# Split weights at eight different distances modulo 256 bytes from the operands they are multiplied with

## The chip, the cores and the metric

The kernel runs on one core of a Trainium2 chip. The metric is the device time in microseconds of one execution. Smaller is better. The core has a matrix engine (TensorE, PE in the profile, with its weight loads as PEld), three engines for elementwise work (VectorE or DVE, ScalarE or ACT, GpSimd or POOL) and a queue that issues transfers (SyncE or SP). Operands lie in an on-chip memory of 128 partitions; a tile occupies the same bytes of every partition, so its place is one start address in bytes.

## The reference

One block of a streaming encoder, on x of 256 tokens by 2048 features, all in float32:

```python
x = x + 0.5 * swiglu(rms_norm(x, ffn1_norm), ffn1_w_up, ffn1_w_down)     # 2048 -> 2 x 5632 -> 2048
h = rms_norm(x, mix_norm)
q_a, f_a, i_a, g_a, x_b, gate_b, gates = split(h @ w_in)
y_a = rms_norm(hgrn2(q_a, f_a, i_a)) * silu(g_a)                         # gated linear recurrence
y_b = rglru(conv4(x_b)) * gelu(gate_b)                                   # scan over the tokens
g = sigmoid(gates + b_gate)
x = x + (g[0] * (y_a @ w_branch_a) + g[1] * (y_b @ w_branch_b)) @ w_out
x = x + cross_attention(rms_norm(x), rms_norm(mem), wq, wkv, wo)         # 4 heads, 256 memory tokens
x = x + 0.5 * swiglu(rms_norm(x, ffn2_norm), ffn2_w_up, ffn2_w_down)
return rms_norm(x, final_norm)
```

Nearly all of the work is products of x or something made of it (256 rows) with large weight matrices, each of which is read once from DRAM.

## The kernel before, in words

**Split products.** TensorE multiplies a type called float32r here, which is faster than float32 and keeps fewer bits. To keep float32's accuracy each operand is split in two: a high part, which is the operand rounded to float32r (`h`, written by ScalarE, L155), and a low part, the operand less its high part (`l`, written by VectorE, L156). A product of A and B is then high x high + low x high + high x low, summed in the accumulators. The operands made of x are split once and kept: `xh` and `xl` in the feed-forward stages, `ops` in the middle, where the two parts lie side by side in one tile, `hidop` for the hidden layer.

**Weight tiles.** A weight tile is 128 partitions by 2048 elements, 8192 bytes per partition. `prepare` (L277) loads it into a tile `raw` and splits it into `h` and `l`. There are three buffers for `raw`, three for `h`, three for `l`, used in turn. Two tiles are prepared ahead of their use (`weights`, L237). In the feed-forward stages, most of the up-projection goes by a scheme of seven products in place of eight (`PRODUCTS`, kind "fast"): it needs differences of weight blocks beside the blocks, in a second pair of tiles. Their high part `th` comes from the pool of `h`, their low part `tl` from a pool `wide`, which exists in these two stages alone (three buffers in the first, two in the second). `wide` also holds the differences before they are split (`td`, first stage) and the evicted accumulators (`ev`). For some tiles the low part is made by a transfer that adds: ScalarE writes -raw and a transfer of GpSimd's queue adds the source (L273, L274 and L312, L313).

**Who is streamed and who is loaded.** A matmul has one operand that is loaded into the array ahead of it (LDWEIGHTS, 128 columns) and one that is streamed through it (256 or 512 columns). In the feed-forward stages (`three`, L562: lines 566, 567 and 569) and in `rows_product` (L352: lines 357, 358 and 360) the operand of x is loaded and 512 columns of weights are streamed. In `product` (L324: lines 332 and 335) the weights are loaded and the operand of x is streamed, 512 columns (both of its parts) against `h`, 256 against `l`. The two lines with `h` always come first, eight to sixteen matmuls in a row, then those with `l`.

```python
for acc, (ah, al), (bh, bl), start, _ in products:
    pe.matmul(acc, ah, bh, start=start, stop=False)    # L566
    pe.matmul(acc, al, bh, start=False, stop=False)    # L567
...
    pe.matmul(acc, ah, bl, start=False, stop=stop)     # L569
```

**Places in memory.** Pools are laid out one behind another in the order in which they are opened: `const`, `raw`, `h`, `l`, `slots` (22 tiles of 4096 bytes, which hold all operands of x), `small`, and behind them the pools of a stage. A tile takes its own size, in steps of 32 bytes. The first tile of `raw` starts at byte 20096, which is 128 more than a multiple of 256. All tiles behind it are multiples of 1024 bytes, with the exception of `small`, whose tiles fill 512 bytes (with the padding `PAD` in them, L451). So in the built program every `raw`, `h`, `l`, `tl`, `td`, `ev`, `xh`, `xl`, `xd`, `ops` and `hidop` starts at 128 modulo 256, and so does every slice of them that a matmul reads, since slices are multiples of 512 bytes apart. The distance from an operand of x to a weight tile, modulo 256, is 0 in all of them. Two other tiles that the prediction uses: the constant `ones` starts at 2784, which is 224 modulo 256; the tile `osq`, in a pool of the middle stage, at 128.

**Order.** The order in which each engine works is fixed when the program is built; addresses have no part in it.

## Time and profile before

| | |
|---|---|
| median of the runs | 2417.88 us (2417.07 to 2418.68, 2 runs) |
| the profiled execution | 2418.76 us |
| its span, first to last instruction | 2417.0 us |
| granted TensorE clock, mean | 0.999 |
| DMA over the span | 684.33 MB, 283 GB/s on average |

The span is the time between the first and the last instruction of the trace; the execution's own time is 1.8 us longer. In the page and in the answers of the trace a row names the line of the kernel, the engine, the operation, and what it writes and reads (`acc<-h,xh` writes an accumulator from `h` and `xh`). Behind `x` stands how many there were, behind the bar the busy time in us and the mean length of one in ns, then the idle time before them and who ended it. A timeline's row begins with the start and the length in us; rows of equal instructions are merged and their number is given. The rows by stretch give the stretch, its length, and for PE, PEld, DVE, ACT and POOL the busy time with the number of instructions, then the granted clock, the DMA engines' busy share and GB/s.

### The profile page before, as it was taken

How to read it: one execution, taken by the hardware profiler on the slowest of the kernel's cores; microseconds unless marked ns; L12 is line 12 of the kernel's file. 1: busy time of each engine (PE TensorE's matmuls, PEld its weight loads, DVE VectorE, ACT ScalarE, POOL GpSimd, SP SyncE). 2: the span in 40 equal slices, each digit the busy share in tenths (PEclk: the TensorE clock that was granted, in tenths of full speed). 3: DMA queues.
4: the chain of work that ended last, by engine and by line, in shares of the span. 5: the costliest groups of instructions: out<-in, count | busy, mean ns of one | idle time of the engine just before them, and what ended most of it. 6: DMA issues, size and time to landing. Idle time of an engine off the chain costs nothing.

```text
span 2417.0 us, 30834 instructions
## 1 busy us (share of the span) xinstructions
PE 2405.1 (100%) x12116; PEld 2006.3 (83%) x12116; DVE 2044.6 (85%) x2275; ACT 1468.6 (61%) x1499; POOL 102.3 (4%) x166
## 2 busy tenths in 40 slices
PE   9999999999999999999999999999999999999998
PEld 8888888888888888888888888888888788888887
DVE  6999999999866878678876787777789999999995
ACT  8566777777654454476434555545676666666664
POOL 0000000000000000000000000000000000000000
PEclk9999999999999999999999999999999999999999
DMA  8578999999858776878989899876788877787773
GB/s 305 203 227 258 276 277 278 273 275 271 270 215 318 276 285 240 302 269 324 353 323 348 291 358 344 324 286 244 265 344 308 292 283 279 269 287 279 285 282 140
DMA packets 102386, 684.33 MB, mean 283 GB/s; under 512 B 11360, under 2 KB 11616, under 8 KB 29280
## 3 DMA queue, kind: packets, MB, share of 16 engines
q1 hardware_dynamic: 78192, 518.68, 57.5%
q0 software_dynamic: 23328, 162.54, 22.4%
q8 instruction: 95, 1.56, 0.2%
q10 hardware_dynamic: 720, 1.13, 0.1%
q14 instruction: 51, 0.42, 0.0%
HBM read 619.39 MB, written 62.91 MB: 282 GB/s over the span
## 4 chain that ended last, share of the span: by engine, by line
PE 97%; DVE 1%; ACT 1%; DMA 1%; issue 0%; ACTq 0%
PE acc L566 18%; PE acc L567 18%; PE acc L569 18%; PE acc L332 11%; PE acc L357 8%; PE acc L358 8%; PE acc L360 8%; PE acc L335 6%; PE acc L607 1%; PE acc L496 1%; ACT h L155 1%; DVE l L156 0%; PE acc L904 0%; DMA raw<-wd 0%; PE acc L1197 0%; PE acc L1151 0%
## 5 line engine op out<-in xcount | busy, mean ns | idle before, releaser
L155 ACT ACTIVATE h<-raw 128x2048 fp32r<-128x2048 f32 (+3 forms) x578 | 867.6, 1526 | 618.8 <-PE acc L358 209.5
L156 DVE TENSOR_TENSOR l<-raw,h 128x2048 fp32r<-128x2048 f32 (+2 forms) x406 | 833.8, 2056 | 209.3 <-ACT h L155 206.3
L566 PE MATMUL acc<-h,xh 128*128 128x512 f32 x1228 | 478.4, 392 | 0.5 <-ACT h L155 0.5
L567 PE MATMUL acc<-h,xl 128*128 128x512 f32 x1228 | 476.1, 390 | 0.0
L357 PE MATMUL acc<-h,ops 128*128 128x512 f32 x832 | 326.8, 393 | 0.0
L358 PE MATMUL acc<-h,ops 128*128 128x512 f32 x832 | 324.6, 390 | 0.0
L332 PE MATMUL acc<-ops,h 128*128 128x512 f32 x1152 | 278.0, 393 | 0.0
L566 PE MATMUL acc<-h,hidop 128*128 128x512 f32 x704 | 276.3, 392 | 1.5 <-ACT h L155 1.5
L566 PEld LDWEIGHTS acc<-h,xh 128*128 128x128 f32 x1228 | 230.5, 188 | 54.4 <-ACT h L155 6.2
L567 PE MATMUL acc<-h,hidop 128*128 128x512 f32 x704 | 274.4, 390 | 0.0
L567 PEld LDWEIGHTS acc<-h,xl 128*128 128x128 f32 x1228 | 230.6, 188 | 46.7
L332 PEld LDWEIGHTS acc<-ops,h 128*128 128x128 f32 x1152 | 211.6, 188 | 41.6
L156 DVE TENSOR_TENSOR tl<-raw,h 128x1024 fp32r<-128x1024 f32 x172 | 203.7, 1220 | 13.8 <-ACT h L155 13.3
L360 PE MATMUL acc<-l,ops 128*128 128x512 f32 x832 | 205.8, 389 | 0.0
L155 ACT ACTIVATE h<-td 128x1024 fp32r<-128x1024 f32 x140 | 146.6, 1055 | 82.6 <-DVE td L304 31.5
L569 PE MATMUL acc<-l,hidop 128*128 128x512 f32 x704 | 190.5, 389 | 0.0
L360 PEld LDWEIGHTS acc<-l,ops 128*128 128x128 f32 x832 | 156.2, 188 | 32.4
L357 PEld LDWEIGHTS acc<-h,ops 128*128 128x128 f32 x832 | 156.2, 188 | 32.3
L358 PEld LDWEIGHTS acc<-h,ops 128*128 128x128 f32 x832 | 156.3, 188 | 31.5
L569 PE MATMUL acc<-tl,xh 128*128 128x512 f32 x624 | 178.1, 392 | 0.1
L156 DVE TENSOR_TENSOR tl<-td,h 128x1024 fp32r<-128x1024 f32 x140 | 170.1, 1220 | 8.3 <-ACT h L155 7.4
L569 PE MATMUL acc<-l,xh 128*128 128x512 f32 x604 | 166.5, 390 | 0.0
(245 smaller groups left out, 2750.5 us busy)
## 6 DMA issues: line engine op xcount, KB each, us to landing
raw<-wu SPq DMA_DIRECT2D x114, 1024.0 KB, 6.3
raw<-wd SPq DMA_DIRECT2D x88, 1024.0 KB, 6.5
prep<-wu POOLq DMA_DIRECT2D x58, 1024.0 KB, 6.5
t<-prep POOLq DMA_DIRECT2D x58, 1024.0 KB, 5.7
raw<-t SPq DMA_DIRECT2D x58, 1024.0 KB, 7.1
raw<-wu SPq DMA_DIRECT2D x58, 768.0 KB, 4.8
raw<-win SPq DMA_DIRECT2D x40, 1024.0 KB, 4.9
raw<-wg SPq DMA_DIRECT2D x32, 1024.0 KB, 5.1
```

The lines of the kernel that those rows point to most:

```text
L155: done["high"] = act.activation(h, raw, ACT.Copy).ins
L156: done["low"] = dve.tensor_tensor(out=l, in0=raw, in1=h.bitcast(F32), op=ALU.subtract).ins
L332: pe.matmul(acc, h[:, k * P:(k + 1) * P], xs[k], start=k == 0, stop=False)
L335: done["product"] = pe.matmul(acc[:, :T], l[:, k * P:(k + 1) * P], xs[k][:, :T], start=False, stop=k == KT - 1).ins
L357: pe.matmul(accs[t], x[:, t * P:][:, :P], h[j], start=first and j == 0, stop=False)
L358: pe.matmul(accs[t], x[:, T + t * P:][:, :P], h[j], start=False, stop=False)
L360: done["product"] = pe.matmul(accs[t], x[:, t * P:][:, :P], l[j], start=False, stop=last and j == 3).ins
L496: pe.transpose(acc[:, z * T + t * P:][:, :P], tile[:, t * 512 + (2 * y + z) * P:][:, :P], ident)
L566: pe.matmul(acc, ah, bh, start=start, stop=False)
L567: pe.matmul(acc, al, bh, start=False, stop=False)
L569: pe.matmul(acc, ah, bl, start=False, stop=stop)
L607: pe.transpose(acc[:, z * T + t * P:][:, :P], hid[t][:, (2 * y + z) * P:][:, :P], ident)
```

## The change

Every weight tile gets 8 elements (32 bytes) more than it uses, so that the buffers of a pool lie 8224 bytes apart in place of 8192 and each starts 32 bytes later modulo 256 than the one before. The new function `full` makes such a tile and returns its first 2048 columns. Small tiles that nobody reads (`between`, `before`, `after`) put the pools that follow at the wanted place. All other tiles stay at 128 modulo 256.

| buffers | start modulo 256 before | after | distance from the operands of x after |
|---|---|---|---|
| the three of `h` (`h`, `th`) | 128, 128, 128 | 128, 160, 192 | 0, 32, 64 |
| the three of `l` | 128, 128, 128 | 224, 0, 32 | 96, 128, 160 |
| the three of `wide` (`tl`, `td`, `ev`) | 128, 128, 128 | 64, 96, 128 | 192, 224, 0 |
| operands of x, `raw`, all else | 128 | 128 | 0 |

In the second feed-forward stage `wide` has its first two buffers alone. On every engine the instructions, their order and their waits are the same in both programs.

```diff
 PAD = 16
+APART = 8
...
     lp = pool("l", 3)
+    pool("between", 1).tile([P, 16], F32, name="between")
     slots = pool("slots", 22)
...
+    def full(pool, name, dt=F32R, tag=None):
+        return pool.tile([P, 2048 + APART], dt, name=name, tag=tag or name)[:, :2048]
...
     def split_tiles():
-        return hp.tile([P, 2048], F32R, name="h", tag="h"), lp.tile([P, 2048], F32R, name="l", tag="l")
+        return full(hp, "h"), full(lp, "l")
...
-        l = lp.tile([P, 2048], F32R, name="l", tag="l")
+        l = full(lp, "l")
...
-            h = hp.tile([P, 2048], F32R, name="h", tag="h")
+            h = full(hp, "h")
...
-                td = scoped["wide"].tile([P, 2048], F32, name="td", tag="wide")
+                td = full(scoped["wide"], "td", F32, "wide")
...
-        th = hp.tile([P, 2048], F32R, name="h", tag="h")
+        th = full(hp, "h")
         if "wide" in scoped:
-            tl = scoped["wide"].tile([P, 2048], F32R, name="tl", tag="wide")
+            tl = full(scoped["wide"], "tl", tag="wide")
         else:
-            tl = lp.tile([P, 2048], F32R, name="tl", tag="l")
+            tl = full(lp, "tl", tag="l")
...
-    FFN1_POOLS = dict(wide=3, hd=1, xd=2, raw1=1)
-    FFN2_POOLS = dict(wide=2, raw2=2, hid=1, hd=1)
+    FFN1_POOLS = dict(before=1, wide=3, after=1, hd=1, xd=2, raw1=1)
+    FFN2_POOLS = dict(before=1, wide=2, after=1, raw2=2, hid=1, hd=1)
...
-                            ev = scoped["wide"].tile([P, 2048], F32, name="ev", tag="wide")
+                            ev = full(scoped["wide"], "ev", F32, "wide")
...
     with scope(**FFN1_POOLS):
+        scoped["before"].tile([P, 48], F32, name="before")
+        scoped["after"].tile([P, 56], F32, name="after")
         ffn("ffn1", pairs1, sq1, to_mix)
...
     with scope(**FFN2_POOLS):
+        scoped["before"].tile([P, 48], F32, name="before")
+        scoped["after"].tile([P, 64], F32, name="after")
         ffn("ffn2", pairs2, sq4, to_out, late, sums2)
```

## The prediction

> **What bounds the kernel now.** I read the page's busy times, the clock row and the chain that ended last first.

> ```profile
> span 2417.0 us, 30834 instructions
> ...
> PE 2405.1 (100%) x12116; PEld 2006.3 (83%) x12116; DVE 2044.6 (85%) x2275; ACT 1468.6 (61%) x1499; POOL 102.3 (4%) x166
> ...
> PEclk9999999999999999999999999999999999999999
> ...
> PE 97%; DVE 1%; ACT 1%; DMA 1%; issue 0%; ACTq 0%
> ```

> TensorE has a matmul in flight in every slice, at the full clock, and 97% of the chain is matmuls. So the kernel lasts as long as its matmuls take from start to start, and only a change of that interval, or a new wait in front of them, can move the end. The rows of the groups say which matmuls these are (the number behind the bar is the mean length of one, which overlaps the next and is not the interval):

> ```profile
> L566 PE MATMUL acc<-h,xh 128*128 128x512 f32 x1228 | 478.4, 392 | 0.5 <-ACT h L155 0.5
> ...
> L332 PE MATMUL acc<-ops,h 128*128 128x512 f32 x1152 | 278.0, 393 | 0.0
> ...
> L335 PE MATMUL acc<-ops,l 128*128 128x256 f32 x1152 | 150.5, 283 | 0.0
> ```

> The interval stands in the timeline. A piece of the second feed-forward stage:

> ```profile
> 2016.73 0.39 PE L566 MATMUL acc<-h,xh 128*128 128x512 f32 x1
> ...
> 2019.68 0.39 PE L567 MATMUL acc<-h,xl 128*128 128x512 f32 x1
> ```

> Thirteen steps in 2019.68 - 2016.73 = 2.95 us: **0.2269 us** for one matmul of 512 columns. The matmuls of 256 columns in the middle of the program:

> ```profile
> 914.80 3.14 PE L332 MATMUL acc<-ops,h 128*128 128x512 f32 x13
> 917.78 2.08 PE L335 MATMUL acc<-ops,l 128*128 128x256 f32 x16
> 919.69 1.55 PE L332 MATMUL acc<-ops,h 128*128 128x512 f32 x6
> ```

> Sixteen in 919.69 - 917.78 = 1.91 us, 0.1194 us each. From 256 to 512 columns the interval grows by 0.1075 us, so 512 columns alone account for 0.215 us and some 0.012 us per matmul do not depend on its columns. Every matmul is preceded by a weight load that starts while the one before it streams:

> ```profile
> 2018.32 0.39 PE L567 MATMUL acc<-h,xl 128*128 128x512 f32 x1
> 2018.33 0.19 PEld L566 LDWEIGHTS acc<-h,xh 128*128 128x128 f32 x1
> ```

> Those 0.012 us are what a change of addresses could touch: at 10 ns after the matmul's start the load begins to read one operand while the matmul reads the other, and in the kernel before both lie at the same place modulo 256 bytes.

> **The change part by part.** No instruction is added, removed or moved, and no wait: on each engine the built program lists the same instructions with the same waits; only start addresses differ. By the program's list of addresses, of 10,668 matmuls with a weight tile 2,310 keep the distance 0, and 8,358 get another: 4,510 with high parts (32 or 64), 3,316 with `l` (96, 128 or 160) and 532 with `tl` (192 or 224, four of them 96). Between one matmul and the next the distance changes 1,499 times, where before it never changes. The terms:

> *The interval at a constant distance other than 0.* No matmul of this type stands in the trace at another distance, so the cost is bounded from both sides. Downward, the nearest rows are plain float32 matmuls, which take two passes' worth of time per column and so stream 256 columns as long as the others 512:

> ```profile
> 1064.38 3.18 PE L1016 MATMUL acc<-xc,lw 128*128 128x256 f32 x14
> ...
> 1028.55 1.02 PE L973 MATMUL acc<-osq,ones 128*128 128x256 f32 x4
> ```

> ```profile
> L1016 PE MATMUL acc<-xc,lw 128*128 128x256 f32 x32 | 7.7, 382 | 0.0
> ...
> L973 PE MATMUL acc<-osq,ones 128*128 128x256 f32 x16 | 4.1, 378 | 0.0
> ```

> L1016: (3.18 - 0.382) / 13 = 0.2152 us; L973: (1.02 - 0.378) / 3 = 0.214 us. So a stream of this length with a weight load beside it can run without the extra: at best 0.2269 - 0.2152 = 11.7 ns are to be had per matmul. The same two rows say something on the distance itself. `xc` and `lw` both lie 128 behind a multiple of 256 (distance 0); `osq` lies at 128 and `ones` at 224 (distance 96). They differ by 1 ns, which is the rounding of these starts. It is the one pair of rows I found with two distances, and it shows no effect, though at half the rate of reading.

> Upward, the longest stretch of slower matmuls with nothing else in the way comes where the pipeline was disturbed a moment earlier:

> ```profile
> 2023.54 0.40 PE L567 MATMUL acc<-h,xl 128*128 128x512 f32 x1
> ...
> 2024.70 0.85 PE L569 MATMUL acc<-l,xh 128*128 128x512 f32 x3
> ```

> Five steps in 1.16 us, 0.232 us each, 5.1 ns more than 0.2269; after that the interval is back. The same shows above behind the change from 256 to 512 columns: thirteen steps from 914.80 to 917.78 take 2.98 us where 13 x 0.2269 are 2.95. So weight load and stream do act on each other, and settle again within some six matmuls. The value I take is **0**: the interval settles to the same value in every stage, whatever the tiles, which is what a load's fixed toll looks like. Both ends are kept for the range: -11.7 ns and +5.1 ns, times 8,358.

> *The 1,499 changes of distance.* From 0 to about 0.03 us each (five steps in 1.16 us instead of 5 x 0.2269 = 1.134, and the sixth unread). I take 0, by the same argument.

> *The splits on ScalarE and VectorE.* They write 32 bytes further and read as before:

> ```profile
> L156 DVE TENSOR_TENSOR l<-raw,h 128x2048 fp32r<-128x2048 f32 x262 | 599.5, 2288 | 206.5 <-ACT h L155 203.5 <-DMA x<-xin 1.1 <-DMA xf<-xT 1.1
> ...
> L156 DVE TENSOR_TENSOR tl<-raw,h 128x1024 fp32r<-128x1024 f32 x172 | 203.7, 1220 | 13.8 <-ACT h L155 13.3
> ```

> 1,024 elements more cost 2288 - 1220 = 1068 ns, 1.043 ns an element, with `raw`, `h` and `l` all at the same place modulo 256. A collision between their two reads would have to show here, at equal distance; the rows leave nothing to win that the path would notice, and what they could lose is a rival below. Cost: 0, hidden beneath TensorE.

> *DMAs.* Source and `raw` tiles keep their alignment; only the added transfers into `l` land elsewhere, on a queue nobody on the path waits for. Cost: 0.

> *Sum.* 2417.0 us of span plus nothing; the profiled execution took 2418.76 us, 0.9 above the median of the runs, 2417.88. Forecast: **2418 us**.

> [...]

> **The rivals.**

> *Faster: the 0.012 us are a collision that needs equal addresses.* The load and the stream start within 10 ns of each other and walk through memory from the same offset. If each such meeting stalls the stream, any other distance frees it: 8,358 x 11.7 ns = 98 us off, 2418 - 98 = **2320 us**; if only some distances are free, in between. For it: the toll does not depend on the columns, as a toll of the load would, and it is larger than in the float32 rows. Against it: reads at different speeds would drift apart and meet at some point whatever the distance, and the value is the same in every stage.

> *Slower: the interval depends on how load and stream stand to each other, and distance 0 is where it is shortest.* The place is L566 to L569, L332 and L357 to L360. If each of the 1,499 changes of distance opens the stretch of longer steps again, 1,499 x 0.03 = 45 us, **2463 us**; if the interval stays long at the 8,358, 8,358 x 5.1 ns = 43 us, 2461 us; both together 2506 us. It ends beyond 2% once a change costs more than 48.4 / 1,499 = 32 ns or a matmul more than 48.4 / 8,358 = 5.8 ns (2.6% of 0.2269). For it: the stretches of longer steps exist, last several matmuls and come without any wait.

> *The other engines lose.* In the first feed-forward stage VectorE has almost no slack:

> ```profile
> 60.00:300.00 240.00, 240.00 (x1072) 197.24 (x1070) 235.06 (x249) 160.05 (x137) 9.72 (x11) 1.00 0.76 242
> 300.00:600.00 300.00, 300.00 (x1334) 245.58 (x1335) 293.96 (x305) 221.25 (x186) 20.94 (x24) 1.00 0.92 274
> ```

> VectorE (the third of the times) is busy 529 of 540 us. Splits 5% slower would need 555 us there and cost up to 15 us, 2433 us. Only a loss above 2% shows at all.

> *The change doesn't do what it says:* a tile's pitch would have to be rounded to more than 32 bytes. The list of addresses says no (44672, 52896, 61120 for the three `h`), so this gets no chance of its own.

> **How the numbers follow.** No effect 0.57; slower by load and stream 0.27, of which 0.18 beyond 2% since its price lies at that bound and reaches 2506; other engines 0.02; faster by a collision 0.14, of which 0.12 beyond 2%. A measurement of this kernel can tell about 2% from no change, so: faster 0.12, within 2% 0.70, slower 0.18. The range reaches up to 2500, which takes in most of the slower case, and down to 2405; the faster case and a tail of the slower stay outside, together 0.2.

> **What the profile after would show.** Right: the timeline steps by 0.227 us in every stage, whatever the weight buffer, and TensorE's groups keep their means (392, 393, 283). The faster rival: steps near 0.215 us with the weight buffers at 32 bytes and more, 0.227 with the first `h` buffer. The slower: steps of 0.23 us and more behind each change from `h` to `l`, or all through a buffer's matmuls; the sorted steps by buffer tell the two apart. If VectorE loses, its mean of 2288 ns rises, by buffer, and matmuls wait for `l` between 60 and 600 us. I am wrong if any distance has a settled interval of its own.

## The result and the profile after

| | before | after |
|---|---|---|
| median of the runs | 2417.88 us | 2452.89 us (2452.41 to 2453.37, 2 runs) |
| ratio, with its 95% interval | | 1.0145 (1.0101 to 1.0188) |
| the profiled execution, its span | 2418.76, 2417.0 us | 2452.41, 2450.6 us |

The change costs 35 us, 1.45%. That is inside the forecast's 2% and inside its range, but the forecast was 2418 us, and the likeliest case was "no effect". So there is a loss to explain.

The page of the changed kernel, the rows that answer to those read before:

```profile
span 2450.6 us, 30834 instructions
...
PE 2439.2 (100%) x12116; PEld 2008.6 (82%) x12116; DVE 2047.2 (84%) x2275; ACT 1470.4 (60%) x1499; POOL 102.3 (4%) x166
...
PEclk9999999999999999999999999999999999999999
...
PE 98%; DVE 1%; DMA 1%; ACT 0%; issue 0%; SPq 0%; ACTq 0%; DVEq 0%
```

The same 30834 instructions and the same granted clock, 0.999 in the mean of both. TensorE's busy time went from 2405.1 to 2439.2 us, 34.1 us more, and its share of the chain from 97% to 98%: it does not wait more (2.9 us on other engines in place of 3.1), its matmuls take longer. VectorE's and ScalarE's busy times stand within 3 us of those before. The groups of the trace by shape say which matmuls (line, engine, operation, what it writes and reads, count, busy us, mean ns of one):

```profile
L571 PE MATMUL acc<-h,xh 128*128 128x512 f32 x1228 | 481.6, 394 | 0.5 <-ACT h L160 0.5
...
L337 PE MATMUL acc<-ops,h 128*128 128x512 f32 x1152 | 281.5, 395 | 0.0
...
L365 PE MATMUL acc<-l,ops 128*128 128x512 f32 x832 | 211.0, 395 | 0.0
...
L340 PE MATMUL acc<-ops,l 128*128 128x256 f32 x1152 | 150.3, 282 | 0.0
```

These are L566, L332, L360 and L335 of the kernel before. The row of L360 there:

```profile
L360 PE MATMUL acc<-l,ops 128*128 128x512 f32 x832 | 205.8, 389 | 0.0
```

The streams of 512 columns are longer by 2 ns (392 to 394, 393 to 395), with `l` by 6 (389 to 395, from 205.8 to 211.0 us in all), those of 256 columns are not (283 to 282). VectorE's largest group did not move (2288 before):

```profile
L161 DVE TENSOR_TENSOR l<-raw,h 128x2048 fp32r<-128x2048 f32 x262 | 599.4, 2288 | 215.6 <-ACT h L160 210.6 <-PE acc L1172 1.8 <-PE acc L340 1.4
```

The two stretches of the first feed-forward stage, with busy time and count for PE, PEld, DVE, ACT and POOL in this order:

```profile
60.00:300.00 240.00, 240.00 (x1055) 194.64 (x1054) 230.51 (x245) 155.56 (x132) 8.85 (x10) 1.00 0.74 235
300.00:600.00 300.00, 300.00 (x1318) 243.15 (x1317) 291.11 (x301) 218.77 (x185) 20.93 (x24) 1.00 0.90 272
```

In the same 540 us TensorE begins 2373 matmuls in place of 2406, and VectorE is busy 521.6 us in place of 529: VectorE now has more idle time than before, 18.4 us in place of 11.

The steps themselves stand in the timeline. A piece of the second feed-forward stage (start and length in us; "x3" merges three):

```profile
2045.82 0.40 PE L571 MATMUL acc<-h,xh 128*128 128x512 f32 x1
...
2047.69 0.85 PE L574 MATMUL acc<-l,xh 128*128 128x512 f32 x3
2048.39 1.09 PE L574 MATMUL acc<-tl,xh 128*128 128x512 f32 x4
2049.32 0.39 PE L571 MATMUL acc<-h,xh 128*128 128x512 f32 x1
...
2050.69 0.39 PE L571 MATMUL acc<-h,xh 128*128 128x512 f32 x1
...
2052.53 0.86 PE L574 MATMUL acc<-l,xh 128*128 128x512 f32 x3
```

By the list of addresses, the eight matmuls from 2045.82 read the `h` buffer at distance 32: (2047.69 - 2045.82) / 8 = **0.2338 us** each. The three with `l` are at 128, 0.233 us; the four with `tl` at 224, 0.2325 us. The six from 2049.32 read the `h` buffer at 64: (2050.69 - 2049.32) / 6 = **0.2283 us**. The eight from 2050.69 are back at distance 0: 1.84 / 8 = **0.2300 us**, and their single steps, from starts in the trace, are 231, 236, 228, 233, 231, 226, 227, 227 ns: they come down to the old interval after five steps. No matmul of these rows waits for anything.

The same for the whole program: each step from a start to the next, put to the distance of the matmul that begins it, against the mean of the same kind in the kernel before (228.99 ns for streamed weights, 230.35 and 120.57 for loaded ones, waits included):

| kind | distance | matmuls | longer by, ns | us |
|---|---|---|---|---|
| weights streamed, 512 columns | 0 | 1926 | 1.68 | 3.2 |
| | 32 | 1928 | 5.69 | 11.0 |
| | 64 | 1814 | 1.88 | 3.4 |
| | 96, 128, 160 | 2167 | 4.35, 3.74, 5.45 | 9.7 |
| | 192, 224 | 528 | 9.36, 3.88 | 3.5 |
| weights loaded, 512 columns | 0, 32, 64 | 1152 | 0.08, 4.42, 4.70 | 3.5 |
| weights loaded, 256 columns | 96, 128, 160 | 1152 | -1.50, 0.91, 0.16 | -0.1 |
| all other work | | | | -0.5 |

The sum is 33.7 us; the spans differ by 33.6. Part of the loss is paid out of waits. Of the streams of 512 columns, the steps over 300 ns (a wait ahead of the next matmul) cost 14.1 us beyond 226.66 ns each in the kernel before and 10.1 us now; the others cost 34.9 us more than before.

### The profile page after: what moved, and what is told of

Same layout as the page of the kernel before. It is cut to its first block, busy times and chain, and to the rows that moved or that the text cites. A ratio compares the mean times of both kernels' runs of the same rounds, so it can differ in the third digit from the quotient of the medians.

```text
span 2450.6 us, 30834 instructions
## 1 busy us (share of the span) xinstructions
PE 2439.2 (100%) x12116; PEld 2008.6 (82%) x12116; DVE 2047.2 (84%) x2275; ACT 1470.4 (60%) x1499; POOL 102.3 (4%) x166
## 4 chain that ended last, share of the span: by engine, by line
PE 98%; DVE 1%; DMA 1%; ACT 0%; issue 0%; SPq 0%; ACTq 0%; DVEq 0%
PE acc L574 18%; PE acc L571 18%; PE acc L572 18%; PE acc L337 11%; PE acc L365 8%; PE acc L362 8%; PE acc L363 8%; PE acc L340 6%; PE acc L612 1%; PE acc L501 1%; PE acc L911 0%; PE acc L1158 0%; PE acc L1204 0%; DMA raw<-t 0%; PE acc L1023 0%; DMA raw<-wu 0%
## 5 line engine op out<-in xcount | busy, mean ns | idle before, releaser
L161 DVE TENSOR_TENSOR tl<-raw,h 128x1024 fp32r<-128x1024 f32 x172 | 203.7, 1219 | 17.3 <-ACT h L160 16.5
L365 PE MATMUL acc<-l,ops 128*128 128x512 f32 x832 | 211.0, 395 | 0.0
L363 PEld LDWEIGHTS acc<-h,ops 128*128 128x128 f32 x832 | 156.3, 188 | 34.1
L161 DVE TENSOR_TENSOR tl<-td,h 128x1024 fp32r<-128x1024 f32 x140 | 170.1, 1220 | 13.5 <-ACT h L160 12.5
```

The costliest lines, as they stand in the source:

```text
L161: done["low"] = dve.tensor_tensor(out=l, in0=raw, in1=h.bitcast(F32), op=ALU.subtract).ins
L363: pe.matmul(accs[t], x[:, T + t * P:][:, :P], h[j], start=False, stop=False)
L365: done["product"] = pe.matmul(accs[t], x[:, t * P:][:, :P], l[j], start=False, stop=last and j == 3).ins
```

## The experiments

Three readings stand against each other. **Settled interval**: each distance has its own interval between starts, whatever came before. **Changes**: distance as such costs nothing, each change of distance opens a stretch of longer steps. **Elsewhere**: the loss comes from the splits, transfers or pools, and the matmuls only show it.

### All weight tiles at one other distance: 32, 64; all pools moved by 256

The kernel before, with pools moved as a whole, so that the distance modulo 256 is the same for every matmul with weights and never changes. No tile gets a new pitch.

```diff
     rawp = pool("raw", 3)
+    pool("between", 1).tile([P, 8], F32, name="between")     # 16 for 64, 64 for 256
     hp = pool("h", 3)
     lp = pool("l", 3)
+    pool("behind", 1).tile([P, 56], F32, name="behind")      # 48 for 64, none for 256
...
     with scope(**FFN1_POOLS):                                # and FFN2_POOLS alike
+        scoped["before"].tile([P, 8], F32, name="before")
+        scoped["after"].tile([P, 56], F32, name="after")
```

> Every weight tile at one and the same distance from the operands of x, 32 bytes modulo 256; no change of distance is left. If each distance has a settled interval of its own (in the trace of the changed kernel the matmuls at distance 32 settle near 233 ns, against 226.4 at 0), about 9,500 matmuls of 512 columns lose 6 to 7 ns each: 2418 + 55 to 65, 2470 to 2485 us. If it is the 1,499 changes of distance that cost, this kernel has none and takes 2418 us.

> As before, all weight tiles at 64 bytes modulo 256. If each distance has its own settled interval: with the weights streamed the changed kernel settles near 229 ns at 64 (2 to 3 ns over distance 0, 8,400 matmuls), with the weights loaded near 233 ns (7 ns, 1,152): 2418 + 20 to 30, 2436 to 2450 us. If the changes of distance cost: 2418 us.

> All weight tiles moved by 256 bytes: 0 modulo 256, but 256 modulo 512, where the kernel before has 0 modulo 512 everywhere. If the place modulo 256 is what counts, 2418 us and intervals of 226.4 ns as before; if the period is longer than 256 bytes, another settled interval and, at 2 to 7 ns each, 2437 to 2485 us.

Measured, one run each on a chip where the kernel before took 2416.74 us: distance 32 **2468.01 us**, distance 64 **2431.32 us**, pools moved by 256 **2417.94 us**. The first two lie a little below what was expected for settled intervals. The group that streams `h` against `xh`, of the kernels with 32 and 64 in this order (L566 of the kernel before, 478.4 us there):

```profile
L568 PE MATMUL acc<-h,xh 128*128 128x512 f32 x1228 | 483.7, 396 | 0.9 <-ACT h L157 0.9
```

```profile
L568 PE MATMUL acc<-h,xh 128*128 128x512 f32 x1228 | 480.2, 393 | 0.3 <-ACT h L157 0.3
```

In the kernel moved by 256 no tile stands behind `l`, so in the built program the operands of x move along with `h` and `l`. What was expected of it, 256 modulo 512, holds for 680 matmuls alone: 620 with `tl` and 60 with `xd`. All others keep the distance 0 modulo 512. The group with `tl`, which took 178.1 us and 392 ns in the kernel before:

```profile
L570 PE MATMUL acc<-tl,xh 128*128 128x512 f32 x624 | 178.1, 391 | 0.0
```

And the timeline at distance 32:

```profile
2047.60 0.40 PE L568 MATMUL acc<-h,xh 128*128 128x512 f32 x1
...
2050.64 0.39 PE L569 MATMUL acc<-h,xl 128*128 128x512 f32 x1
```

Thirteen steps in 3.04 us, 0.2338 us, in the place of 0.2269; the interval never comes back. The distance alone, without one change of it and without a new pitch, costs 51 us at 32 and 15 us at 64. The reading of changes alone falls. So does that of a loss elsewhere: the steps that wait for nothing carry the loss, and moving all pools by 256 bytes costs nothing. At 32 the streamed steps without a wait are 6.66 ns over 226.66 in the mean, 8,285 of them, so 55.2 us where the kernel before had 5.3; the shorter waits give 4.4 back (9.8 us where before had 14.1). The loaded weights add 4.0, which makes the 49 us by which the spans differ. At 64 the loss is smaller, for a second reason beside the shorter interval. Two groups of that kernel:

```profile
L334 PE MATMUL acc<-ops,h 128*128 128x512 f32 x1152 | 283.2, 397 | 0.0
...
L337 PE MATMUL acc<-ops,l 128*128 128x256 f32 x1152 | 144.2, 277 | 0.0
```

With weights loaded, the 512 columns are as slow as at 32 (397 ns in place of 393), but the 256 columns are faster than before, 277 ns in place of 283: by steps 5.5 ns less, 6.3 us in all.

### The interval at each distance

A program that only multiplies: the encoder's block is left out. Two weight tiles fill `W`, the second of them again, with a few words of the first behind it, fills `X`; 48 matmuls in a row of 512 columns of `W`, moved by 4 bytes from one row of 48 to the next, with 128 columns of `X` loaded; then 256 columns; then with roles exchanged; then with both moved together.

```python
for o in range(64):                  run(weights(o), xs())
for o in range(64, 129, 8):          run(weights(o), xs())
for o in range(0, 64, 8):            run(weights(o, 256), xs(), cols=256)
for o in range(0, 64, 8):            run(...)       # X streamed, W moved by o and loaded
for o in range(0, 64, 8):            run(weights(o), xs(o))
```

> Leaves out the whole block; it measures the interval alone: runs of 48 matmuls of 512 columns, the streamed operand starting 0, 4, 8 ... 252 bytes (modulo 256) behind the loaded one, then 256 to 512 in steps of 32, then streams of 256 columns, then the two roles exchanged, then both operands moved together. No other engine works beside it. If distance alone sets the settled interval: 226 to 227 ns at 0, about 233 at 32, 229 at 64, one value per distance, repeated after 256 bytes, and 226 to 227 wherever both are moved together. If other engines' accesses are part of it: 226 to 227 ns at all distances here. Whether a distance under 32 bytes is faster than 0 is open; if the load's toll of 12 ns is a collision, some distance comes down to about 215 ns.

Nothing but TensorE works in these stretches (ScalarE's 7.6 us lie before 11.9 us and behind 1053.4 us), and the granted clock is 1.00 in those at 256, 32 and 64. Pieces of the timeline inside the rows at distance 256, 32, 64 and 20 (each line is one stretch cut out of the trace):

```profile
734.68 7.19 PE L116 MATMUL acc<-W,X 128*128 128x512 f32 x31
```

```profile
107.06 7.63 PE L116 MATMUL acc<-W,X 128*128 128x512 f32 x32
```

```profile
196.36 7.49 PE L116 MATMUL acc<-W,X 128*128 128x512 f32 x32
```

```profile
73.36 7.84 PE L116 MATMUL acc<-W,X 128*128 128x512 f32 x32
```

With 0.39 us for the last: 6.80 / 30 = 0.2267 us at 256, 7.24 / 31 = 0.2335 at 32, 7.10 / 31 = 0.2290 at 64, 7.45 / 31 = 0.2403 at 20. The table has the means of the last 32 steps of each row, from the single starts, in ns. The distance is the streamed operand's place less that of the loaded one; in the last line it is how far the loaded one is moved forward. The value for 0 is that of the rows at 256 and 512 and of the later rows with equal places. The very first row, at 0, begins with steps of 427 ns and still has 227.4 at its end.

| distance | 0 or 256 | 12 | 20 | 32 | 60 | 64 | 96 | 128 | 160 | 192 | 224 | 288 | 320 |
|---|---|---|---|---|---|---|---|---|---|---|---|---|---|
| 512 columns | 226.7 | 229.2 | 240.0 | 233.3 | 228.3 | 229.0 | 233.4 | 233.3 | 234.3 | 233.3 | 233.3 | 233.3 | 228.8 |
| 256 columns | 120.0 | | | 117.8 | | 117.8 | 120.1 | 118.5 | 118.6 | 117.8 | 118.3 | | |
| 512, roles exchanged | 226.7 | | | 233.3 | | 233.3 | 234.4 | 232.6 | 233.4 | 228.8 | 233.3 | | |

- Of the 64 places in steps of 4 bytes, 0 is the shortest for 512 columns, 60 the next with 228.3, and 240.0 the longest (20, 68, 132, 196). None is below 226.66, so there is no collision at 0 that another distance would free.
- The period is 256 bytes: 288 reads like 32, 320 like 64, 512 like 256.
- With the roles exchanged 192 takes the place of 64. What counts is the place of the streamed operand less that of the loaded one, which is why 64 with loaded weights was slow above.
- Both moved together, by 0 to 224 bytes: 226.7 ns in all eight rows. Only the difference counts.
- For 256 columns distance 0 is among the longest of the eight places in the table.

The kernel after agrees with the table: its streamed matmuls from the seventh of a run on, without waits, have 227.4 ns at 0, 233.4 at 32 and 228.9 at 64.

### High parts at 0, low parts of `l` at 64: many changes

The kernel before with `l` moved by 64 bytes. The distance changes 1,030 times, between the best place and the second best of the multiples of 32. The operands of x move too, by 256 bytes, so in this program `h` lies at 256 modulo 512 from them, which is 0 modulo 256.

```diff
     hp = pool("h", 3)
+    pool("between", 1).tile([P, 16], F32, name="between")
     lp = pool("l", 3)
+    pool("behind", 1).tile([P, 48], F32, name="behind")
```

> High parts and tl at distance 0, low parts at 64: no distance here is slow in the runs of one distance (the low parts' 2,168 streams of 512 columns lose 2.3 ns each by those, 5 us, and their 1,152 streams of 256 columns win 2.3 ns each, 3 us), but the distance changes 1,030 times. If only the settled interval of each distance counts: before + 2 us, about 2419 us. If each change costs what a disturbance costs at distance 0 (27 ns by the run with both operands moved): before + 2 + 28, about 2447 us.

Measured: **2435.6 us** against 2418.62 on that chip, 17 us more: between the two, so changes do cost, but less than expected. The groups with `h` against `xh` and `l` against `xh` in this kernel:

```profile
L568 PE MATMUL acc<-h,xh 128*128 128x512 f32 x1228 | 479.4, 392 | 0.4 <-ACT h L157 0.4
...
L571 PE MATMUL acc<-l,xh 128*128 128x512 f32 x604 | 170.3, 395 | 0.0
```

And the second of them in the kernel with all tiles at 64:

```profile
L571 PE MATMUL acc<-l,xh 128*128 128x512 f32 x604 | 167.8, 392 | 0.0
```

`l` is at 64 in both, and yet takes 395 ns here and 392 there: only three matmuls with `l` stand in a row, and they are over before the interval of 64 is reached. One such place, from starts in the trace: three with `l` 236, 235, 232 ns, then four `tl` at distance 0 with 234, 231, 233, 236, then six `h` at 0 with 224, 231, 236, 228, 233, 231, and then 226.7 again. So one excursion of three matmuls lengthens twelve. That `h` comes back to 226.7 at 256 modulo 512 bears out the period of 256. By steps, 6,196 streamed matmuls at 0 lost 1.70 ns each, 10.5 us; 2,167 at 64 lost 4.24, 9.2 us, of which the constant 64 explains 1.63 ns each, 3.5 us. What the changes cost the streamed weights is then 10.5 + 5.7 = 16.2 us, **16 ns** for each of 1,030; counted over the 882 changes that lie between two streamed weights it is 18 ns.

### A narrower load, and rows that alternate

Only matmuls again. 256 columns at all 64 places; 512 columns at distance 0 behind loads of 128, 96, 64 and 32 columns; then 0 alternating with 0, 64 or 128, in eights, in sixteen and eight, and each time.

```python
for m in (128, 96, 64, 32):
    ... pe.matmul(acc[:m], X[:, i % 16 * P:][:, :m], weights(0)(i), ...)
for o, a, b in ((0, 8, 8), (16, 8, 8), (32, 8, 8), (0, 16, 8), (16, 16, 8), (32, 16, 8), (16, 1, 1), (32, 1, 1)):
    run(lambda i: weights(o if i % (a + b) >= a else 0)(i), xs(), n=96)
```

> Leaves out the whole block, as the first run of this kind. [...] Then distances 0 and 64 (and 0 and 128) by turns, every 8, every 16 and 8, and every matmul: if only settled intervals count, the mean of the two; if each change costs 27 ns, 3.4 ns on every matmul at turns of 8.

The four rows with narrower loads, as the timeline merges them:

```profile
380.13 44.30 PE L130 MATMUL acc<-W,X 128*128 128x512 f32 x192
```

Loads of 128, 96, 64 and 32 columns leave 226.7, 230.0, 230.1 and 231.7 ns over the last 32 steps; the mean of all 191 steps is (44.30 - 0.39) / 191 = 0.2299 us. So a load of a quarter of the columns does not shorten the interval, it lengthens it: the 0.012 us are no toll that shrinks with what is loaded.

The rows that alternate, over whole turns, from starts in the trace:

| | interval, ns | mean of the settled values | each change costs, ns |
|---|---|---|---|
| 0 and 64, by eights | 229.6 | 227.8 | 14 |
| 0 and 64, sixteen and eight | 228.6 | 227.4 | 14 |
| 0 and 64, each time | 230.8 | 227.8 | 3 |
| 0 and 128, by eights | 230.4 | 230.0 | 3 |
| 0 and 128, sixteen and eight | 229.2 | 228.9 | 3 |
| 0 and 128, each time | 230.0 | 230.0 | 0 |

Between 0 and 64, with eight matmuls and more at each, a change costs nearly what it cost in the kernel. Between 0 and 128, where 128 itself is slow, it costs next to nothing. So there is no one price of a change.

For 256 columns the best places were 16, 112 and 192 with 113.3 ns; 23 of the 64 lay within 0.1 ns of 120.0. The place 192 had 117.8 in the run before, where it was reached from another place: one place, two intervals. And 113.3 is half of 226.7. At the best places of these two lengths the interval is in proportion to the columns, and no part of it is left that does not depend on them.

### 512 and 256 columns in the kernel's order

In the product with loaded weights, sixteen matmuls of 512 columns at distance 0 are followed by sixteen of 256. Only matmuls: this unit, three times for each of 64 places of the low parts.

```python
for k in range(16): pe.matmul(acc, W[:, k * P:(k + 1) * P], X[:, k % 4 * 512:][:, :512], ...)
for k in range(16): pe.matmul(acc[:, :T], W[:, 2048 + o + k % 15 * P:][:, :P], X[:, k % 4 * 512:][:, :T], ...)
```

> Leaves out the whole block. Sixteen streams of 512 columns at distance 0, then sixteen of 256 columns whose loaded weights lie 0, 4, 8 ... 252 bytes further, three times each, as a unit of the middle stage does it. If the interval of 256 columns follows from the distance alone, the values of the second run of this kind return (120 ns at 0, 113 to 114 at the stream 16, 112 and 192 bytes behind the load, that is the load at 240, 144 and 64). If it also depends on where the sequence comes from, since one and the same distance gave 113.8 ns in one kernel and 117.5 in another, some of these fall away, and the distance that is left is the one to try in the kernel.

The timeline where the place goes from 72 to 76:

```profile
325.42 3.84 PE L129 MATMUL acc<-X,W 128*128 128x512 f32 x16
329.10 2.06 PE L131 MATMUL acc<-X,W 128*128 128x256 f32 x16
330.99 3.83 PE L129 MATMUL acc<-X,W 128*128 128x512 f32 x16
334.66 1.99 PE L131 MATMUL acc<-X,W 128*128 128x256 f32 x16
336.49 3.81 PE L129 MATMUL acc<-X,W 128*128 128x512 f32 x16
```

A unit at 72 takes 330.99 - 325.42 = 5.57 us, one at 76 takes 336.49 - 330.99 = 5.50, and 5.48 from the next on. The sixteen of 256 columns go from 118 to 114 ns each. 76 and 180 were the best with 5480 ns; 0 takes 5566. The places that were best in rows of 256 columns alone are not best here. The weights are the loaded operand now, so 16, 112 and 192 of those rows are 240, 144 and 64 here, and these take 5527, 5560 and 5540. The other way round, 76 here is 180 there, which had 120.0 ns. What 256 columns settle to depends on what ran before them.

### The changed kernel again, and two versions that follow from this

The changed kernel once more beside two others: the kernel before in which only the low parts of loaded weights (L335, 256 columns) lie 76 or 180 bytes further.

```diff
-        plan.extend(((name, i), w[i], "plain") for i in which)
+        plan.extend(((name, i), w[i], "columns") for i in which)
...
-        if kind == "plain":
-            h, l = split_tiles()
+        if kind in ("plain", "columns"):
+            if kind == "columns":
+                h = hp.tile([P, 2048], F32R, name="h", tag="h")
+                l = lp.tile([P, 2048 + 64], F32R, name="l", tag="l")[:, 19:19 + 2048]    # 45: 180 bytes
+            else:
+                h, l = split_tiles()
```

> The changed kernel itself, timed beside the others on one chip: 2452 to 2453 us, 1.4% over before. If the first comparison was off by its own width, between 1.0 and 1.9%.

> The kernel before, with one edit: the low parts of the weights that are loaded in the middle stage (1,152 streams of 256 columns) start 76 bytes further; all streams of 512 columns stay at distance 0. By the sequence run a unit of 16 and 16 matmuls takes 5,480 ns in place of 5,566: 72 units x 86 ns, 6 us less than before, about 2412 us. If the settling in the kernel's own order of tiles goes otherwise, as it did at 64 bytes (2 us), 2416 us.

> The same with 180 bytes, the other distance at which the sequence run gave 5,480 ns a unit: about 2412 us, or 2416 us if the settling goes otherwise in the kernel's own order.

| | median us | ratio to before, 95% |
|---|---|---|
| before | 2417.93 (21 runs) | |
| the changed kernel | 2452.56 (4 runs) | 1.0143 (1.0129 to 1.0157) |
| low parts of loaded weights at 76 | 2412.67 (11 runs) | 0.9977 (0.9968 to 0.9986) |
| the same at 180 | 2412.37 (11 runs) | 0.9976 (0.9967 to 0.9986) |

Two groups of the kernel with 76:

```profile
L336 PE MATMUL acc<-ops,h 128*128 128x512 f32 x1152 | 278.2, 393 | 0.0
...
L339 PE MATMUL acc<-ops,l 128*128 128x256 f32 x1152 | 144.7, 277 | 0.0
```

The 256 columns go from 150.5 to 144.7 us, 283 to 277 ns, and the 512 columns beside them keep 393. By steps the 1,152 lose 5.10 ns each, 5.9 us of the 6.4 by which the spans differ. It is a small gain, but its interval excludes 1, and both versions beat the kernel before.

## Why the prediction was right and where it was wrong

**What held.** TensorE bounds the kernel, and only the interval between starts could move the end: the table by distance adds up to the whole difference. The other engines and the transfers cost nothing: VectorE's group has 2288 ns and DMA 1% of the chain in both. The tiles' pitch is what the change says, and the order of the work did not change. The 2% on either side and the range held the result, but not by the mechanism of the forecast: a loss that it had put at nothing came to 1.45%. That it stayed under 2% is luck. With all tiles at 32 the distance costs 2.1%, 2468.01 us against 2416.74.

**The step that failed** is the first term: "The interval at a constant distance other than 0 ... The value I take is **0**: the interval settles to the same value in every stage, whatever the tiles, which is what a load's fixed toll looks like." In every stage the distance had been the same, 0. That the value came back everywhere was therefore no evidence about other distances; it was one point measured many times. Measured in its place, with nothing but TensorE at work: 233.3 ns at 32, 229.0 at 64, 233 to 234 at 96 to 224, against 226.7. This is the last of the forecast's own signs of being wrong, a settled interval of another distance. Nor are the 0.012 us a fixed toll: they come from 512 columns less 256, and the 256 columns at distance 0, with 120.0 ns, are not at their shortest. At their best places they take 113.3 ns, half of 226.7. The second piece of evidence, the pair of plain float32 rows at distances 0 and 96 with 215 and 214 ns for 256 columns, did not carry over. `osq` is streamed there and `ones` is loaded, so its place by the count of the tables is 160; float32r of 512 columns takes 234.3 at 160 and 233.4 at 96. The reservation "at half the rate of reading" should have set the weight.

**The changes of distance**, taken as 0 to 0.03 us with 0 chosen: 14 to 18 ns each between 0 and 64 where several matmuls stand at each, 3 ns between 0 and 128, so not one addition everywhere. In the changed kernel the streamed matmuls at distance 0 show it by itself: 3.2 us, with 268 returns of streamed weights to 0 in the program about 12 ns for each. Between two slow distances the long steps are there anyway: with all tiles at 32, the first six steps of a run without waits have 232.9 ns and the later ones 233.3. That is why "both together 2506 us" did not come.

**The rivals.** The slower one is what happened: distance 0 is where the interval is shortest, in its variant of an interval that stays long. Its price was 8,358 x 5.1 ns = 43 us. The matmuls with weights became longer by 34.9 + 3.5 - 0.1 = 38.3 us in all, the 3.2 at distance 0 included; shorter waits gave 4.1 us back and all other work 0.5. The price per matmul was an average of unlike things: 5.7 ns at 32, 1.9 at 64, nothing at 256 columns, which had been counted like the others. Nor did the working allow for the waits, which were shorter with the slower TensorE: 10.1 us in place of 14.1. By the table the 8,358 matmuls at other distances cost 30.9 us, 3.7 ns each in place of 5.1, so the 5.8 ns from which it would have ended beyond 2% were not reached. At 32 throughout the 48.4 us that are 2% are crossed (51 us). The faster rival has fallen for 512 columns, since none of 64 places is below 226.66 ns; in small it is true for 256 columns, 114.3 in place of 120 ns, which the forecast had not looked at apart. The other two took no part.

**The chances.** 0.57 for no effect leaned on an argument with no contrast in it; the bound in the prediction's own rows, five steps of 0.232 us, was nearer to the truth than the value chosen (0.2333).

**What stays open.** Why the intervals are what they are, and what the 12 ns are by which distance 0 itself lies above the float32 rows' 215: no run here removed them, and none left the weight loads out. Nor does a run show whether the two operands meet in the memory at all, or what the distance does with another type than float32r.

## What to carry to other kernels

Look at start addresses modulo 256 when a padding or another pool moves tiles: for float32r streams of 512 columns beside weight loads, streamed and loaded operands at the same place gave the shortest interval here, 226.7 ns, and 32 bytes cost 2.9%, 233.3 ns. A value that is the same everywhere is evidence on a cause only if the cause varies between the places; a sweep with nothing but the operation in question makes it vary. For streams of 256 columns the best place was another (113.3 ns at 16, 112 and 192 against 120.0 at 0) and depended on what ran before (behind 512 columns at distance 0, loaded weights 76 and 180 further were best, 5480 ns a unit against 5566), so it is to be measured in the kernel's own order.
